# A smaller DMA scratch area and another SBUF layout in a macaron GLA / gated DeltaNet block

## The chip, the core and the metric

The kernel runs on one core of one Trainium2 chip. The metric is device time in microseconds (us). Engines are named as in the profile: PE (TensorE), DVE (VectorE), ACT (ScalarE), POOL (GpSimd), SP (SyncE); "SPq" in a chain is SP's queue, which issues most of the DMAs.

## The reference

One decoder block for 1,024 tokens and a model width of 1,024, float32:

```python
h = x + 0.5 * swiglu(rms_norm(x, ffn1_norm), ffn1_w_gate, ffn1_w_up, ffn1_w_down)   # inner width 2816
h = h + hybrid_mixer(rms_norm(h, mixer_norm), ...)    # GLA, 4 heads, and gated DeltaNet, 8 heads, merged by gates
h = h + 0.5 * swiglu(rms_norm(h, ffn2_norm), ffn2_w_gate, ffn2_w_up, ffn2_w_down)
return rms_norm(h, final_norm)
```

The DeltaNet part needs, for each head and each chunk of 64 tokens, the inverse of a unit lower triangular matrix that is made of the keys, their decays and beta.

## The kernel before

**Matmuls.** Each float32 product runs as three passes on PE over operands that are split into a high and a low part: ACT casts the high part (L119, L125), DVE or POOL subtracts the low part (L120, L126). Weights come from HBM as 128x512 tiles `raw`, and are split into `wh` and `wl` (`load_unit`, L108). The feed forwards use Strassen products over blocks of 512 (`strassen_products`, L310), whose combined activation blocks are the tiles t2h to t4l (h and l for the two parts); the activations between up and down projection are in tiles ah and al.

**Stages in the trace.** First feed forward: 0 to about 735 us. DeltaNet, one head after the other: to about 1370 us. GLA: to about 1865 us. Output projection, second feed forward and final norm: to the end.

**One DeltaNet head.** The masked, decayed key products are put into `lt` (L905 to L914) and go to DRAM as `l_d` (SP, L914), and come back in a layout with 128 blocks of 32x32 (SP, L917). POOL inverts them by 31 steps of a multiply and a subtract (L924, L927), copies the transpose (L929), and stores both to DRAM tensor `x_d` by eight DMAs that it issues itself:

```python
        for a in range(4):
            r, c = slice(32 * a, 32 * a + 32), slice(8 * a, 8 * a + 8)
            nc.gpsimd.dma_start(out=x_d[0, :, :, c], in_=xp[r])
            nc.gpsimd.dma_start(out=x_d[1, :, c, :], in_=xt[r])
```

L932 stores a 32-partition part of `xp` so that each run of contiguous bytes in `x_d` is 8 floats, 32 bytes: 1,024 runs, 32 KB. L933 stores as many bytes in runs of 8x32 floats, 1 KB: 32 runs. SP then loads them as `xb` and `yb` (L944, L945), and PE goes on from 32x32 to 64x64 blocks (`delta_levels`, L972). SP's queue holds, behind these loads, the ones of the next head: `gb` (L840, that head's cumulated decays, from `g_d`), two `raw` tiles, and `eye` into `xp` (L919). From `gb` comes the decay matrix `em` (L837 on), from that `l_d`.

**Other DMAs that POOL issues.** Eight stores of the residual to `h_d` after the first feed forward (L702), and eight loads from it before the output projection (L1356), 128 runs of 4 KB each.

**SBUF and order.** Tiles lie in pools on a stack with two ends. From the left: `const`, `xn` (normed activations), `wp` (raw x2, wh x4, wl x4), and then per stage other pools: h1 (the residual ha) and t1 (all else of the first feed forward); `me`, mx and on the right mp, sp, mb, ma in the mixer; h2 (h0 to h7) and t2 for the second feed forward. A tile that is first written where an earlier pool's tiles lay waits for the last users of just those tiles (`reuse_waits="tile"`). The order of each engine's instructions is set by a scheduler from priorities and from these waits, so that another layout can give another order.

**At the start of the mixer** POOL clears n1, xb, yb (L769) and yi (L1195); DVE and ACT copy a first projection from PSUM into yi (L1197, L1198); DVE forms the decays of all heads in yi by 16 scans of 64 tokens (L773, called at L1217), and SP stores them as `g_d` (L1219). **At its end** the loads of h0 to h7 (L1356) go to addresses of the closed mixer pools, and DVE adds the output projection to h (L281).

Of the kernel before, what the change touches and what calls it, by code (L numbers as in the profile page):

```python
# [7 lines left out]
F32 = mybir.dt.float32  # L8
F32R = mybir.dt.float32r
# [6 lines left out]
P = 128  # L16
T = 1024
# [31 lines left out]
def tile_macaron_hybrid(  # L49
# [20 lines left out]
    dram = ctx.enter_context(tc.tile_pool(name="dram", bufs=1, space=DRAM))  # L70
    xn = ctx.enter_context(tc.tile_pool(name="xn", bufs=1))
    wp = ctx.enter_context(tc.tile_pool(name="wp", bufs=4))

    nc.scalar.preload_act_table_set("sqrt_and_others")
    cs = const.tile([P, C_TRI], F32, name="cs")
# [32 lines left out]
    def load_unit(src, keep=None, stage=None):  # L108
        res = []
        for hf in range(2):  # L110
            raw = stage() if stage else wp.tile([P, 512], F32, name="raw", tag="raw", bufs=2)
            nc.sync.dma_start(out=raw, in_=src[:, hf * 512:hf * 512 + 512])
            if keep is None:
                wh = wp.tile([P, 512], F32R, name="wh", tag="wh")
                wl = wp.tile([P, 512], F32R, name="wl", tag="wl")
            else:
                wh, wl = keep[:, 0, hf], keep[:, 1, hf]
            with tc.high_priority(offset=400):
                nc.scalar.copy(out=wh, in_=raw)  # L119
# [187 lines left out]

    recent = []

    def strassen_products(tp, xs, tmp, corner, raws, place=bank, pool_steps=3):  # L310
        comb = {}

        def tile512(n):
# [1 line left out]

        def sums_own():
            for c in ("t2", "t3", "t4"):
                comb[c] = [tp.tile([P, 4, 512], F32R, name=c + p, tag=c + p) for p in "hl"]
            for k in range(4):
                def join(out, r, sl, eng):  # L320
                    eng.tensor_add(out=out, in0=xs[r][0][:, sl].bitcast(F32), in1=xs[r][1][:, sl].bitcast(F32))
                    return out

                b12 = join(corner(), k, HI, nc.vector)
                b22 = join(tile512("c11"), k + 4, HI, nc.vector)
                b11 = join(tile512("c21"), k, LO, nc.vector)
# [94 lines left out]

        return sums_own, sums_inplace, strassen

    def ffn(h, xs, wg, wu, wd, tp, ysc, first, last, pre, steps, after):
        def act_tiles():
            return [tp.tile([P, T], F32R, name=n, tag=n, bufs=2) for n in ("ah", "al")]

        def gate_up(j):
            gps, ups = ptile(), ptile()
            if j == 0:  # L430
                dense_pair(((gps, load_unit(wg[j]), P), (ups, load_unit(wu[j], stage=stage), P)), xs, first, pre, steps,
                           ((4,), (1, 5)), len(first) - 1)
            else:
                dense(gps, load_unit(wg[j]), xs)
                dense(ups, load_unit(wu[j]), xs)
            a = s_tile(tp)
            if j == 0:
                b = tp.tile([P, T], F32, name="al", tag="al", bufs=2)
                with tc.high_priority(offset=400):
                    nc.scalar.copy(out=a, in_=gps)  # L440
                    nc.scalar.copy(out=b, in_=ups)
                gps, ups = a, b
            nc.vector.tensor_mul(out=a, in0=ysc, in1=gps)
            nc.scalar.activation(out=a, in_=a, func=AF.Silu)
            nc.vector.tensor_mul(out=a, in0=a, in1=ysc)
            done[:] = [nc.vector.tensor_mul(out=a, in0=a, in1=ups).ins]
            nc.sync.dma_start(out=a_d[j], in_=a)
# [5 lines left out]
            return tp.tile([P, 512], F32, name="sr", tag="sr", bufs=2)  # L453

        def raws():
            return ([wp.tile([P, 512], F32, name="raw", tag="raw", bufs=2) for _ in range(2)] +
                    [stage() for _ in range(2)])

        def weight_sum():
            return tp.tile([P, 512], F32, name="wt", tag="wt", bufs=2)  # L460

        sums_own, sums_inplace, strassen = strassen_products(tp, xs, weight_sum, weight_sum, raws, pool_steps=2)

        def gate_up2(j):
            ss = [s_tile(tp), s_tile(tp)]
# [59 lines left out]
        def chunk_ops(c):  # L525
            names = ("b11", "b21", "t2", "t3", "t1", "t4", "b22")
            res = {}
            for i, n in enumerate(names):
                if c % 2:
                    res[n] = [[t[:, k] for k in range(2)] for t in  # L530
                              (xn.tile([P, 2, 512], F32R, name=f"x{p}{i}", tag=f"x{p}{i}") for p in "hl")]
                elif i < 6:
                    m = ("t2h", "t2l", "t3h", "t3l", "t4h", "t4l")[i]
                    t = tp.tile([P, 4, 512], F32R, name=m, tag=m)
                    res[n] = [[t[:, 2 * p + k] for k in range(2)] for p in range(2)]
                else:
                    res[n] = [[tp.tile([P, 512], F32R, name=m, tag=m, bufs=bf) for m, bf in q]
                              for q in ((("c11", 1), ("c21", 1)), (("c22", 1), ("wt", 2)))]
            return res

        def prepare(c, ops, first=None):
            parts = [first] if first else []
            for k in range(len(parts), 2):
                ss = [tp.tile([P, T], F32, name=n, tag=n, bufs=2) for n in (("ah", "al") if k and c else ("s", "s"))]
                for i in range(2):
                    nc.sync.dma_start(out=ss[i], in_=a_d[DCH[c][2 * i + k]])
                parts.append(ss)
# [1 line left out]
                yield from part_steps(k, parts[k], ops)  # L549

        def down(u, ops, h0, h1, steps):
            r1 = wp.tile([P, 512], F32, name="raw", tag="raw", bufs=2)
            r2 = tp.tile([P, 512], F32, name="sr", tag="sr", bufs=2)
            for i, t in enumerate((r1, r2)):
                nc.sync.dma_start(out=t, in_=u[:, i * 512:i * 512 + 512])
# [54 lines left out]
        sums_own()  # L610
        gate_up(1)
        with tc.issue_after(done[0]):
            at = [tp.tile([P, T], F32, name="ah", tag="ah", bufs=2) for _ in range(2)]
            for i in range(4):
                sums_inplace(i, lambda eng: at[i % 2][:, (LO, HI)[i // 2]])
        for j in range(2, NF - 4, 2):
# [19 lines left out]
        acts = []  # L636
        kept = []
        for n in ("t2h", "t2l"):
            t = tp.tile([P, 4, 512], F32R, name=n, tag=n).rearrange("p (j a) t -> p j (a t)", j=2)
# [7 lines left out]
        prev = (tail, acts)  # L647
        sqrt_table()
        ns = norm_space(tp)
        held = hold(wd, prev[0], tp)  # L650
        for seg in last:
            accumulate(wd, *prev, h, 0.5, seg, held=held)
            after(seg, ns)
# [6 lines left out]
        return st.enter_context(tc.tile_pool(name=name, bufs=bufs, reuse_waits="tile", **kw))  # L660

    with ExitStack() as st:
        hp = pool(st, "h1")
        tp = pool(st, "t1")
        ha = hp.tile([P, KT, T], F32, name="ha")
# [24 lines left out]
        def between(seg, ns):  # L690
            steps = norm_steps(h, seg, P_MX, xs2, ns)
            if seg[0] == 0:
# [6 lines left out]
        ffn(h, xs, g1, u1, d1, tp, ysc, FIRST, HALVES, begin1, None, between)  # L699
        with tc.high_priority(offset=-4000):  # L700
            for k in range(KT):
                nc.gpsimd.dma_start(out=h_d[:, k], in_=ha[:, k])  # L702

    with ExitStack() as st:
        with ExitStack() as stm:
            ys, h = mixer(stm, st, tc, pool, start, xs2, load_unit, dense, ptile, bank, rsqrt_newton, split, new_x,
                           accumulate, block_units(OBLOCKS), dram, pr, ident, ones, cst, eye, wlr, win,
                           wout, y_d, h_d, sqrt_table, strassen_products, wp, psum, divide, recent, pinned, run)
# [4 lines left out]
        held = hold(wout, units, tp)  # L713
# [20 lines left out]
        ffn(h, xs, g2, u2, d2, tp, ysc, HALVES, LAST, None, steps, finish)  # L734


def mixer(st, sto, tc, pool, start, xs, load_unit, dense, ptile, bank, rsqrt_newton, split, new_x, accumulate,
          ounits, dram, pr, ident, ones, cst, eye, wlr, win, wout, y_d, h_d, sqrt_table, strassen_products, wp, psum, divide, recent, pinned, run):
    nc = tc.nc
    mp = pool(st, "mp", side="right")  # L740
    sp = pool(st, "sp", 3, side="right")
# [503 lines left out]
    for i in range(8):  # L1245
# [28 lines left out]
        if i < 4:  # L1274
            nc.sync.dma_start(out=y_d[ORDER[i]], in_=outs[i])
    sums_own, sums_inplace, strassen = strassen_products(
        mx, xs, lambda: wp.tile([P, 512], F32, name="raw", tag="raw", bufs=2),
        lambda: wp.tile([P, 512], F32, name="raw", tag="raw", bufs=2),
        lambda: [mx.tile([P, 512], F32, name="sr", tag="sr", bufs=4) for _ in range(4)],
        lambda: psum("m", 512), 2)  # L1280
    sums_own()
# [68 lines left out]
        split(raw[t], *ys[t])  # L1350
    str_.close()
    stl.close()
    hp = pool(sto, "h2")
    h = [hp.tile([P, T], F32, name=f"h{k}", tag=f"h{k}") for k in range(KT)]
    for k in range(KT):
        nc.gpsimd.dma_start(out=h[k], in_=h_d[:, k])  # L1356
    accumulate(wout, ounits[0], ys[:4], h, 1.0)
    sqrt_table()
    return ys, h


def _units(w):
# [83 lines left out]
```

## Time and profile before

| | |
|---|---|
| median of 3 runs | 2672.56 us (2671.76 to 2674.8) |
| profiled execution, its own time | 2674.82 us |
| its span in the trace | 2672.4 us |
| PE busy | 2503.4 us, 94% of the span |
| DVE, ACT, POOL busy | 70%, 40%, 42% |

The span is what the trace covers; the execution's own time is 2.4 us longer. Engines overlap, so their shares don't add up. The chain of waits follows the last instruction back to what released it, step by step, and so tells which work set the time.

### The profile page before, as it was taken

To read this page: it belongs to the slowest core of one execution; us is meant where nothing else is said; L and a number is where in the kernel's file an instruction comes from. 1 tells how busy PE (TensorE), PEld (TensorE's weight loads), DVE (VectorE), ACT (ScalarE), POOL (GpSimd) and SP (SyncE) were. 2 spreads that over 40 slices of the span, in tenths; PEclk is the share of its full clock that TensorE was granted. 3 is DMA by queue.
4 is the path that set the end of the run, shared out by engine and by line. 5 is a ranking of instruction groups with operands and counts; after the bars stand their busy time and mean duration, and the time that the engine had idled before them with its cause. 6 is when DMAs were issued, how large, how long until landed. Compare 5 with 4: busy or idle time off the path is not lost.

```text
span 2672.4 us, 32776 instructions
## 1 busy us (share of the span) xinstructions
PE 2503.4 (94%) x11656; PEld 2019.5 (76%) x11656; DVE 1869.0 (70%) x2907; ACT 1066.5 (40%) x1845; POOL 1113.9 (42%) x1200
## 2 busy tenths in 40 slices
PE   7899999899997988889989999999989999998998
PEld 6788888667776767667767787877768888886677
DVE  8755556999686767667586757766586555558996
ACT  5333334333352434344345544545233333343331
POOL 4544444653327444445452212221154444446541
PEclk9999999999998999999999999999999999999999
DMA  3222221322222222212211212122312222213222
GB/s 114 79 73 82 83 91 60 112 79 91 98 81 52 60 56 59 60 48 56 63 50 37 80 43 84 40 84 87 122 32 76 68 87 87 87 60 115 79 87 80
DMA packets 118051, 199.04 MB, mean 74 GB/s; under 512 B 37208, under 2 KB 43096, under 8 KB 117888
## 3 DMA queue, kind: packets, MB, share of 16 engines
q1 hardware_dynamic: 111376, 184.04, 21.5%
q0 software_dynamic: 4352, 10.49, 1.5%
q10 hardware_dynamic: 2160, 2.43, 0.3%
q8 instruction: 91, 1.49, 0.2%
q14 instruction: 72, 0.59, 0.1%
HBM read 158.73 MB, written 38.17 MB: 74 GB/s over the span
## 4 chain that ended last, share of the span: by engine, by line
PE 60%; DVE 16%; POOL 9%; issue 5%; DMA 4%; ACT 4%; SPq 2%; POOLq 0%; DVEq 0%; ACTq 0%
PE q L367 28%; PE m L367 10%; PE ps L138 10%; PE q L573 6%; POOL xp L927 4%; POOL itmp L924 3%; DVE wl L126 3%; DVE xl L126 1%; DVE ha L578 1%; DVE h L578 1%; PE q L902 1%; PE q L981 1%; DMA s<-a_d 1%; DVE xl L238 1%; DMA gb<-g_d 1%
## 5 line engine op out<-in xcount | busy, mean ns | idle before, releaser
L126 DVE TENSOR_TENSOR wl<-raw,wh 128x512 fp32r<-128x512 f32 x244 | 200.2, 821 | 172.0 <-ACT wh L125 170.5
L138 PE MATMUL ps<-xl,wh 128*128 128x512 f32 (+2 forms) x736 | 254.8, 405 | 20.2 <-ACT wh L119 8.3
L126 DVE TENSOR_TENSOR wl<-sr,wh 128x512 fp32r<-128x512 f32 x232 | 204.7, 882 | 76.2 <-ACT wh L125 75.9
L138 PE MATMUL ps<-xh,wh 128*128 128x512 f32 (+2 forms) x736 | 254.4, 405 | 0.0
L138 PE MATMUL ps<-xh,wl 128*128 128x512 f32 (+2 forms) x736 | 254.2, 403 | 0.1
L367 PE MATMUL q<-xh,wl 128*128 128x512 f32 x640 | 249.4, 390 | 0.0
L367 PE MATMUL q<-xh,wh 128*128 128x512 f32 x640 | 249.3, 390 | 0.0
L367 PE MATMUL q<-xl,wh 128*128 128x512 f32 x640 | 249.2, 389 | 0.0
L125 ACT CAST wh<-sr 128x512 fp32r<-128x512 f32 x232 | 143.7, 619 | 244.7 <-PE q L573 61.9
L924 POOL TENSOR_TENSOR itmp<-lt,xp 128x112 f32<-128x112 f32 (+29 forms) x248 | 114.9, 463 | 255.1 <-DMA lt<-l_d 226.1
L472 POOL TENSOR_TENSOR s<-s,ysc 128x512 f32<-128x512 f32 x80 | 112.6, 1418 | 247.8 <-ACT s L471 247.8
L125 ACT CAST wh<-raw 128x512 fp32r<-128x512 f32 x244 | 144.9, 594 | 176.2 <-PE q L367 100.5
L138 PEld LDWEIGHTS ps<-xl,wh 128*128 128x128 f32 (+1 forms) x736 | 137.8, 191 | 51.7 <-DVE xl L238 9.1
L355 POOL TENSOR_TENSOR raw<-sr 128x512 f32<-128x512 f32 x20 | 27.5, 1375 | 328.6 <-DMA sr<-in_win 235.8
L138 PEld LDWEIGHTS ps<-xh,wh 128*128 128x128 f32 (+1 forms) x736 | 138.8, 192 | 24.6 <-issue 0.8
L138 PEld LDWEIGHTS ps<-xh,wl 128*128 128x128 f32 (+1 forms) x736 | 137.4, 191 | 23.7 <-issue 1.0
L378 DVE TENSOR_TENSOR c<-c,q 128x512 f32<-128x512 f32 x120 | 82.4, 686 | 84.8 <-PE q L367 84.6
L367 PEld LDWEIGHTS q<-xl,wh 128*128 128x128 f32 x640 | 120.2, 188 | 26.2
L367 PEld LDWEIGHTS q<-xh,wl 128*128 128x128 f32 x640 | 120.1, 188 | 25.5
L367 PEld LDWEIGHTS q<-xh,wh 128*128 128x128 f32 x640 | 120.1, 188 | 25.3
L373 ACT COPY c<-q 128x512 f32<-128x512 f32 x120 | 70.5, 588 | 162.2 <-PE q L367 161.7
L927 POOL TENSOR_TENSOR xp<-xp,itmp 128x112 f32<-128x112 f32 (+29 forms) x248 | 120.9, 488 | 19.4
(483 smaller groups left out, 6780.8 us busy)
## 6 DMA issues: line engine op xcount, KB each, us to landing
sr<-in_win SPq DMA_DIRECT2D x80, 256.0 KB, 2.6
a_d<-s SPq DMA_DIRECT2D x36, 512.0 KB, 3.7
raw<-in_win SPq DMA_DIRECT2D x66, 256.0 KB, 2.6
raw<-in_d SPq DMA_DIRECT2D x56, 256.0 KB, 2.6
raw<-in_g SPq DMA_DIRECT2D x48, 256.0 KB, 2.6
s<-a_d SPq DMA_DIRECT2D x24, 512.0 KB, 4.2
sr<-in_u SPq DMA_DIRECT2D x44, 256.0 KB, 2.7
raw<-in_u SPq DMA_DIRECT2D x44, 256.0 KB, 2.6
```

What stands on the lines that cost most here:

```text
L125: a = nc.scalar.copy(out=hi, in_=src)
L126: b = (eng or nc.vector).tensor_sub(out=lo, in0=src, in1=hi.bitcast(F32))
L138: mm = nc.tensor.matmul(out=ps[:m, sl], lhsT=w[:, :m], rhs=x[:, sl], start=(i == 0 and a == 0), stop=(i == n - 1 and a == 2))
L355: nc.gpsimd.tensor_tensor(out=o, in0=a, in1=b, op=op)
L367: nc.tensor.matmul(out=ps, lhsT=p[:, c], rhs=q, start=(first and k == 0 and a == 0), stop=(k == 3 and a == 2), skip_group_check=not first)
L373: marks[0] = nc.scalar.copy(out=t, in_=ps).ins
L378: marks[1] = nc.vector.tensor_add(out=t, in0=t, in1=ps).ins
L472: nc.gpsimd.tensor_mul(out=s, in0=s, in1=y)
L573: nc.tensor.matmul(out=ps, lhsT=p[:, c], rhs=q, start=(first and k == 0 and a == 0), stop=(k == 1 and a == 2), skip_group_check=not first)
L578: nc.vector.scalar_tensor_tensor(out=hd[:, sl], in0=ps, scalar=0.5, in1=hd[:, sl], op0=ALU.mult, op1=ALU.add)
L924: inv_eng.tensor_tensor(out=tv, in0=lp[:, j, j + 1:].unsqueeze(2).broadcast_to([P, r, m]), in1=xp[:, j, :m].unsqueeze(1).broadcast_to([P, ...
L927: inv_eng.tensor_tensor(out=xv, in0=xv, in1=tv, op=ALU.subtract)
```

## The change

Three things:

- The two `raw` tiles move from the left end (`wp`) to a new pool `rp` at the right end.
- The tiles t2h to t4l, ah and al of both feed forwards move from t1 and t2 into new pools q1 and q2 (`tq`), which are opened before h1 and h2. They then lie directly above `wp`, and ha or h0 to h7 above them.
- The program is built with `dynamic_dma_scratch_size=2048`, where the default is 16384. This is an area at the bottom of each SBUF partition which is kept for DMAs that POOL issues. Everything on the left moves down by 14,336 bytes.

In the mixer `me` now covers what t2h to t4l, ah and al left, and the right-hand pools with yi cover what ha left. Between the mixer's left and right pools 12 KB per partition are now covered by neither; h0 to h2 lie there.

```diff
     wp = ctx.enter_context(tc.tile_pool(name="wp", bufs=4))
+    rp = ctx.enter_context(tc.tile_pool(name="rp", bufs=2, side="right"))
...
-            raw = stage() if stage else wp.tile([P, 512], F32, name="raw", tag="raw", bufs=2)
+            raw = stage() if stage else rp.tile([P, 512], F32, name="raw", tag="raw", bufs=2)
...
-                comb[c] = [tp.tile([P, 4, 512], F32R, name=c + p, tag=c + p) for p in "hl"]
+                comb[c] = [(tq or tp).tile([P, 4, 512], F32R, name=c + p, tag=c + p) for p in "hl"]
...
-            return [tp.tile([P, T], F32R, name=n, tag=n, bufs=2) for n in ("ah", "al")]
+            return [tq.tile([P, T], F32R, name=n, tag=n, bufs=2) for n in ("ah", "al")]
...
     with ExitStack() as st:
+        tq = pool(st, "q1")
         hp = pool(st, "h1")
...
     stl.close()
+    tq = pool(sto, "q2")
     hp = pool(sto, "h2")
...
-    nc = _bacc.Bacc("TRN2", target_bir_lowering=False, num_devices=1)
+    nc = _bacc.Bacc("TRN2", target_bir_lowering=False, num_devices=1, dynamic_dma_scratch_size=2048)
```

Line numbers of the changed kernel are larger by 1 to 4 (L702 is L705 there, L769 L772, L773 L776, L914 L917, L917 L920, L932 L935, L1195 L1198, L1356 L1360). The order of instructions is the same on all engines but for the program's first 80 us and the first heads of the mixer. ACT has two rows more, both loads of its function tables.

POOL where the mixer starts, before: the memsets of three tiles that were cleared at L769 (one of them, n1, is printed as n_5770) and of yi stand behind the last stores of the residual and the last splits (xl) of the normed activations.

```order
L702 DMA h_d<-ha 128x1024 x3
L126 TENSOR_TENSOR xl_5419<-c_5224,xh_5418 128x512
L126 TENSOR_TENSOR xl_5429<-c_5226,xh_5428 128x512
L126 TENSOR_TENSOR xl_5439<-c_5225,xh_5438 128x512
L126 TENSOR_TENSOR xl_5449<-c_5224,xh_5448 128x512
L769 MEMSET n_5770 128x1024
L769 MEMSET xb 128x1024
L769 MEMSET yb 128x1024
L1195 MEMSET yi 128x1024
L924 TENSOR_TENSOR itmp<-lt,xp 128x31
```

And now:

```order
L705 DMA h_d<-ha 128x1024 x2
L772 MEMSET n_5777 128x1024
L772 MEMSET xb 128x1024
L772 MEMSET yb 128x1024
L705 DMA h_d<-ha 128x1024
L127 TENSOR_TENSOR xl_5425<-c_5230,xh_5424 128x512
L127 TENSOR_TENSOR xl_5435<-c_5232,xh_5434 128x512
L127 TENSOR_TENSOR xl_5445<-c_5231,xh_5444 128x512
L127 TENSOR_TENSOR xl_5455<-c_5230,xh_5454 128x512
L1198 MEMSET yi 128x1024
L927 TENSOR_TENSOR itmp<-lt,xp 128x31
```

The three memsets stand ahead of the last store and the last splits; yi's comes right behind the splits.

DVE some 10 us later, before: the last of the 16 scans into yi (L773), between rows of the first head's convolution (acc, kq).

```order
L773 SCALAR_TENSOR_TENSOR yi<-cs,oT 8x64 x12
L120 TENSOR_TENSOR wl<-raw,wh 128x512
L791 SCALAR_TENSOR_TENSOR acc<-ps,ph,acc 128x511
L773 SCALAR_TENSOR_TENSOR yi<-cs,oT 8x64
L791 SCALAR_TENSOR_TENSOR acc<-ps,ph,acc 128x510
L773 SCALAR_TENSOR_TENSOR yi<-cs,oT 8x64
L791 SCALAR_TENSOR_TENSOR acc<-ps,ph,acc 128x509
L773 SCALAR_TENSOR_TENSOR yi<-cs,oT 8x64 x2
L1231 TENSOR_SCALAR beta<-q 128x8x4
```

And now, the last 11 rows up to the last scans (L776):

```order
L776 SCALAR_TENSOR_TENSOR yi<-cs,oT 8x64 x6
L830 SCALAR_TENSOR_TENSOR kq_5789<-sig,acc 128x4x128
L794 SCALAR_TENSOR_TENSOR acc<-ps,ph,acc 128x512
L776 SCALAR_TENSOR_TENSOR yi<-cs,oT 8x64
L794 SCALAR_TENSOR_TENSOR acc<-ps,ph,acc 128x512
L776 SCALAR_TENSOR_TENSOR yi<-cs,oT 8x64
L794 SCALAR_TENSOR_TENSOR acc<-ps,ph,acc 128x512
L121 TENSOR_TENSOR wl<-raw,wh 128x512
L776 SCALAR_TENSOR_TENSOR yi<-cs,oT 8x64 x3
L830 SCALAR_TENSOR_TENSOR kq_5789<-sig,acc 128x4x128
L776 SCALAR_TENSOR_TENSOR yi<-cs,oT 8x64 x2
```

The scans are spread over more of the convolution's rows: ahead of the last of them stand rows (acc, kq, wl) which stood behind it.

SP behind the store of the decays (`g_d`), before:

```order
L1219 DMA g_d<-yi 8x1024
L840 DMA gb<-g_d 128x1024 x2
L112 DMA raw<-in_win 128x512 x2
L914 DMA l_d_6018<-em 32x8x32 x4
L112 DMA raw<-in_win 128x512
L917 DMA lt<-l_d_6018 32x1024 x4
```

And now:

```order
L1222 DMA g_d<-yi 8x1024
L843 DMA gb<-g_d 128x1024 x2
L113 DMA raw<-in_win 128x512
L917 DMA l_d_6025<-em 32x8x32 x4
L113 DMA raw<-in_win 128x512 x2
L920 DMA lt<-l_d_6025 32x1024 x4
```

The weights' `raw` loads stand elsewhere: one before the store of `l_d` and two between it and the loads of `lt`, where there were two and one.

## Rows read from the trace of the kernel before

**Rows 1.** The page: PE's busy time (part 1) and the chain by engine (part 4).
```profile
PE 2503.4 (94%) x11656; PEld 2019.5 (76%) x11656; DVE 1869.0 (70%) x2907; ACT 1066.5 (40%) x1845; POOL 1113.9 (42%) x1200
...
PE 60%; DVE 16%; POOL 9%; issue 5%; DMA 4%; ACT 4%; SPq 2%; POOLq 0%; DVEq 0%; ACTq 0%
```

**Rows 2.** Windows, one delta head: us, then busy us (instructions) per engine, PEclk, DMA share, GB/s.
```profile
1019.00:1089.00 70.00, 63.07 (x344) 50.99 (x343) 51.81 (x112) 30.02 (x57) 35.82 (x72) 0.98 0.22 57
```

**Rows 3.** Chain of waits, 944 to 1036 us: start us, us, what.
```profile
947.90 1.02 POOL xt L929
...
952.50 2.95 DMA x_d<-xp
...
961.10 5.03 DMA gb<-g_d
...
974.17 2.13 DVE em L908 x8
...
1023.13 2.67 DMA x_d<-xp
```

**Rows 4.** Timeline of POOL, 946 to 954 us: start us, us, engine, line, operation.
```profile
948.75 0.78 POOL L932 DMA_DIRECT2D x_d<-xp  x1
949.52 0.50 POOL L933 DMA_DIRECT2D x_d<-xt  x1
...
952.50 0.87 POOL L932 DMA_DIRECT2D x_d<-xp  x1
```

**Rows 5.** Lines L932 and L933: ns min/median/max to issue; last, time to landing.
```profile
L932 POOL DMA_DIRECT2D x_d<-xp x32: 759/806/871, 823.8 to 1299.6; - x32
...
DMA to landing us min/median/max: 2.6/2.7/4.4
...
L933 POOL DMA_DIRECT2D x_d<-xt x32: 502/540/615, 824.6 to 1300.3; - x32
...
DMA to landing us min/median/max: 2.0/2.1/3.9
```

**Rows 6.** Chain of waits near x_d of heads 1, 2, 7, 8.
```profile
827.64 2.72 DMA x_d<-xp
...
877.95 0.69 PE ps L138 x3
...
1233.36 0.70 DVE h L1038
...
1299.58 2.73 DMA x_d<-xp
```

**Rows 7.** Timelines of POOL and DVE, and waits of PE, 740 to 748 us.
```profile
742.55 0.96 POOL L1195 MEMSET yi<- 128x1024 f32 x1
...
743.55 0.69 DVE L1197 COPY yi<-ps 72x512 f32<-72x512 f32 x1 [0.67 <-POOL yi L1195]
...
PE ps L138 <- ACT yi L1198: 1.3, 1, 1.3
```

**Rows 8.** Timelines of SP and POOL, 760 to 791 us.
```profile
762.80 0.34 SPq L1219 DMA_DIRECT2D g_d<-yi  x1
...
778.61 1.82 SPq L914 DMA_DIRECT2D l_d<-em  x4
...
782.72 1.70 SPq L917 DMA_DIRECT2D lt<-l_d  x4
...
787.61 0.24 POOL L924 TENSOR_TENSOR itmp<-lt,xp 128x31 f32<-128x31 f32 x1 [44.10 <-DMA lt<-l_d]
```

**Rows 9.** Timelines of POOL, DVE and PE, 1872 to 1882 us.
```profile
1875.12 4.29 POOL L1356 DMA_DIRECT2D h<-h_d  x8 [26.94 <-DVE xl L126]
...
1879.44 1.22 DVE L281 SCALAR_TENSOR_TENSOR h<-ps,h 128x1024 f32<-128x1024 f32 x1 [2.59 <-DMA h<-h_d]
...
1880.82 0.70 PE L138 MATMUL ps<-xl,wh 128*128 128x512 f32 x2 [2.77 <-DVE h L281]
```

**Rows 10.** ACT's table loads at L1209, in the groups by line.
```profile
L1209 ACT ACT_TABLE_LOAD x1 | 1.3, 1283 | 0.0
```

More of the change, by code (lines that the diff above doesn't have):

```diff
@@ L308, in tile_macaron_hybrid, with strassen_products @@
     recent = []
-    def strassen_products(tp, xs, tmp, corner, raws, place=bank, pool_steps=3):
+    def strassen_products(tp, xs, tmp, corner, raws, place=bank, pool_steps=3, tq=None):
         comb = {}
@@ L422, in strassen_products, with ffn @@
         return sums_own, sums_inplace, strassen
-    def ffn(h, xs, wg, wu, wd, tp, ysc, first, last, pre, steps, after):
+    def ffn(h, xs, wg, wu, wd, tq, tp, ysc, first, last, pre, steps, after):
         def act_tiles():
-            return [tp.tile([P, T], F32R, name=n, tag=n, bufs=2) for n in ("ah", "al")]
+            return [tq.tile([P, T], F32R, name=n, tag=n, bufs=2) for n in ("ah", "al")]
         def gate_up(j):
@@ L437, in gate_up @@
             if j == 0:
-                b = tp.tile([P, T], F32, name="al", tag="al", bufs=2)
+                b = tq.tile([P, T], F32, name="al", tag="al", bufs=2)
                 with tc.high_priority(offset=400):
@@ L455, in raws @@
         def raws():
-            return ([wp.tile([P, 512], F32, name="raw", tag="raw", bufs=2) for _ in range(2)] +
+            return ([rp.tile([P, 512], F32, name="raw", tag="raw", bufs=2) for _ in range(2)] +
                     [stage() for _ in range(2)])
@@ L460, in weight_sum @@
             return tp.tile([P, 512], F32, name="wt", tag="wt", bufs=2)
-        sums_own, sums_inplace, strassen = strassen_products(tp, xs, weight_sum, weight_sum, raws, pool_steps=2)
+        sums_own, sums_inplace, strassen = strassen_products(tp, xs, weight_sum, weight_sum, raws, pool_steps=2, tq=tq)
         def gate_up2(j):
@@ L533, in chunk_ops @@
                     m = ("t2h", "t2l", "t3h", "t3l", "t4h", "t4l")[i]
-                    t = tp.tile([P, 4, 512], F32R, name=m, tag=m)
+                    t = tq.tile([P, 4, 512], F32R, name=m, tag=m)
                     res[n] = [[t[:, 2 * p + k] for k in range(2)] for p in range(2)]
@@ L543, in prepare @@
             for k in range(len(parts), 2):
-                ss = [tp.tile([P, T], F32, name=n, tag=n, bufs=2) for n in (("ah", "al") if k and c else ("s", "s"))]
+                ss = [p.tile([P, T], F32, name=n, tag=n, bufs=2)
+                      for p, n in (((tq, "ah"), (tq, "al")) if k and c else ((tp, "s"), (tp, "s")))]
                 for i in range(2):
@@ L551, in down @@
         def down(u, ops, h0, h1, steps):
-            r1 = wp.tile([P, 512], F32, name="raw", tag="raw", bufs=2)
+            r1 = rp.tile([P, 512], F32, name="raw", tag="raw", bufs=2)
             r2 = tp.tile([P, 512], F32, name="sr", tag="sr", bufs=2)
@@ L612, in ffn @@
         with tc.issue_after(done[0]):
-            at = [tp.tile([P, T], F32, name="ah", tag="ah", bufs=2) for _ in range(2)]
+            at = [tq.tile([P, T], F32, name="ah", tag="ah", bufs=2) for _ in range(2)]
             for i in range(4):
@@ L638, in ffn @@
         for n in ("t2h", "t2l"):
-            t = tp.tile([P, 4, 512], F32R, name=n, tag=n).rearrange("p (j a) t -> p j (a t)", j=2)
+            t = tq.tile([P, 4, 512], F32R, name=n, tag=n).rearrange("p (j a) t -> p j (a t)", j=2)
             kept.append([t[:, k] for k in range(2)])
@@ L649, in ffn @@
         ns = norm_space(tp)
-        held = hold(wd, prev[0], tp)
+        held = hold(wd, prev[0], tq)
         for seg in last:
@@ L698, in between @@
                        steps=steps)
-        ffn(h, xs, g1, u1, d1, tp, ysc, FIRST, HALVES, begin1, None, between)
+        ffn(h, xs, g1, u1, d1, tq, tp, ysc, FIRST, HALVES, begin1, None, between)
         with tc.high_priority(offset=-4000):
@@ L705, in tile_macaron_hybrid @@
         with ExitStack() as stm:
-            ys, h = mixer(stm, st, tc, pool, start, xs2, load_unit, dense, ptile, bank, rsqrt_newton, split, new_x,
+            ys, h, tq = mixer(stm, st, tc, pool, start, xs2, load_unit, dense, ptile, bank, rsqrt_newton, split, new_x,
                            accumulate, block_units(OBLOCKS), dram, pr, ident, ones, cst, eye, wlr, win,
-                           wout, y_d, h_d, sqrt_table, strassen_products, wp, psum, divide, recent, pinned, run)
+                           wout, y_d, h_d, sqrt_table, strassen_products, rp, psum, divide, recent, pinned, run)
         tp = pool(st, "t2")
@@ L712, in tile_macaron_hybrid @@
         units = block_units(OBLOCKS)[1]
-        held = hold(wout, units, tp)
+        held = hold(wout, units, tq)
         ysc = tp.tile([P, T], F32, name="ysc", tag="ysc")
@@ L732, in finish @@
                 (nc.sync if k % 2 else nc.scalar).dma_start(out=out[k, :, sl], in_=o)
-        ffn(h, xs, g2, u2, d2, tp, ysc, HALVES, LAST, None, steps, finish)
+        ffn(h, xs, g2, u2, d2, tq, tp, ysc, HALVES, LAST, None, steps, finish)
 def mixer(st, sto, tc, pool, start, xs, load_unit, dense, ptile, bank, rsqrt_newton, split, new_x, accumulate,
-          ounits, dram, pr, ident, ones, cst, eye, wlr, win, wout, y_d, h_d, sqrt_table, strassen_products, wp, psum, divide, recent, pinned, run):
+          ounits, dram, pr, ident, ones, cst, eye, wlr, win, wout, y_d, h_d, sqrt_table, strassen_products, rp, psum, divide, recent, pinned, run):
     nc = tc.nc
@@ L1276, in mixer @@
     sums_own, sums_inplace, strassen = strassen_products(
-        mx, xs, lambda: wp.tile([P, 512], F32, name="raw", tag="raw", bufs=2),
-        lambda: wp.tile([P, 512], F32, name="raw", tag="raw", bufs=2),
+        mx, xs, lambda: rp.tile([P, 512], F32, name="raw", tag="raw", bufs=2),
+        lambda: rp.tile([P, 512], F32, name="raw", tag="raw", bufs=2),
         lambda: [mx.tile([P, 512], F32, name="sr", tag="sr", bufs=4) for _ in range(4)],
@@ L1358, in mixer @@
     sqrt_table()
-    return ys, h
+    return ys, h, tq
 def _units(w):
```

## Prediction

> **What bounds the kernel now.** I read the page first: PE is busy for 94% of the span, but the chain that ended last lies on PE for 60% alone [rows 1]. So there are stretches in which something else sets the time, and a transfer or a wait there counts in full. Then I went by windows along the span. In one DeltaNet head of 70 us PE works 63.1 us and POOL 35.8 us [rows 2]: nobody is full, which is how a closed loop looks. The chain of waits shows the loop [rows 3]: POOL ends the inverse and copies the transpose; POOL issues the eight stores to x_d; the last `xp` store takes 2.95 us to land; SP, which waits for it, issues the loads of xb and yb and only behind them `gb` of the next head, 5.03 us; DVE makes `em`; `l_d` and `lt` go through DRAM; POOL inverts again, and about 70 us after the one landing stands the next. Every delay on POOL or at a landing is then a delay of the next head.
>
> The chain also holds the x_d landings of the heads 1 and 8, and, with the same rows as these, 3 to 6; at head 2 it runs through PE, at head 7 through DVE and ACT [rows 6]. So six of the eight heads pass their delay on, and two have slack of a size that the chain does not show.
>
> **The scratch area.** The change cuts by eight what SBUF holds for DMAs that POOL issues. The rows tell that POOL writes something for each piece of such a DMA: L932 and L933 move 32 KB each, one in 1,024 runs of 32 bytes, the other in 32 runs of 1 KB, and cost POOL 806 and 540 ns [rows 5]. With the large area nothing waits for room. The four L932 of a head start 1.25 us apart (948.75 to 952.50 in three steps [rows 4]), while each needs 2.7 us to land [rows 5], so at each start but the first one or two others are still under way. No row shows what POOL does when room runs out. Bounds:
>
> - Nothing waits, because the pieces still fit: 0.
> - An L932 waits until the L932 before it has landed: four starts 2.7 us apart instead of 1.25, so the last one starts 3 x 1.45 = 4.35 us later. Call it 4.3 us per head.
> - Every one of the eight waits for the one before: three pairs of 2.7 + 2.1 us and one L932 until the last L933 starts, 17.1 us after the first start instead of 4.6: 12.5 us per head.
>
> I take the middle. L932 is by far the finest cut of POOL's transfers: 1,024 runs over 16 DMA engines are 64 for each, and 2,048 bytes are 32 bytes for each of these 64. If a piece takes more than 16 of them, the area holds one L932 and not two, and the second has to wait for the first, as the chosen case has it; at less, two fit, the first is nearly home when the third starts (2.7 us against 2 x 1.25), and nothing waits. That a piece needs a source, a target and a length makes the first the likelier to me. L933 brings two runs per engine and takes hardly any room, so it need not wait for itself. Six heads make 6 x 4.3 = 25.8 us; with bounds of 0 and, with all eight heads, 34.4 us (the third bullet, 6 x 12.5 = 75 us, I leave outside as unlikely).
>
> [...]
>
> POOL's other transfers, L702 and L1356, have eight runs per engine, 128 of 4 KB over 16, and I cost them at nothing: the stores of h_d are waited for much later, and the loads fall under the next but one part.
>
> **The start of the mixer.** In the trace POOL clears three tiles and then yi at 742.55, DVE waits 0.67 us for that, and PE 1.3 us for ACT's copy into yi [rows 7]. Now the three memsets come ahead of the last splits, and yi's stands 2.7 us earlier (three memsets of about 0.9 us). That gain holds only if yi sets what comes next. What it leads to is the decays: scans, `g_d` at 762.80, `l_d` at 778.61, `lt` at 782.72, POOL's first inverse at 787.61 [rows 8]. In the changed order DVE puts several convolution rows ahead of the last scans, and SP puts two `raw` loads instead of one between `l_d` and `lt`, the second of which needs DVE's split of an older tile. I walked the changed DVE rows with the durations of before and got the last scan 4 to 5 us later than now; I take 4.5 us, with bounds of -2.7 us (the early yi carries through) and +5 us. That goes into the first head's loop, on which the landing at 827.64 of [rows 6] lies, in full. ACT's two further table loads, at 1.28 us each [rows 10], are one before the first norm's square root and one ahead of the first tanh here, where ACT has room; 0, at most 1.3 us for each.
>
> **The end of the mixer.** POOL issues the eight loads of h only at 1875.12, after waiting 26.94 us for a split on DVE whose input lay on the same addresses; h0 lands some 4 us later, DVE adds at 1879.44 and PE, which waits for the freed PSUM, stands for 2.77 us [rows 9]. Now h0 to h2 lie where neither pool of the mixer lay, and their loads wait for nothing there. DVE can add as soon as its last split is done (1876.85, the 1879.44 less the 2.59 us it waited). Gain 2.6 us, with bounds of 0 (the next load or the order of DVE eats it) and 2.8 us. The loads come earlier beside others that have several us to spare; I cost that at nothing, and should it fail, the bound of 0 is it.
>
> All the rest keeps its order: the Strassen products of both feed forwards, the heads from the fourth on, GLA, and the final norm. Moving `raw` to the other end changes no count of buffers.
>
> **The sum.** The profiled execution took 2674.8 us, 2.4 more than its span, and 2.3 more than the median of the runs. 2674.8 + 25.8 + 4.5 - 2.6 = 2702.5; against the median 2672.6 that is 2700.3. I predict **2700 us** for a median. This case's own range: at least five heads (21.5) with nothing lost at the start and 2.8 gained at the end, 2691; at most eight heads (34.4), 5 at the start, two table loads (2.6) and no gain at the end, 2714.6, of which I give 2713.
>
> **Rivals.** A measurement of this kernel tells about 0.2%, 5.3 us, from no change.
>
> - *The pieces still fit, or POOL writes ahead without waiting.* Then only the ends of the mixer count: 2672.6 + 4.5 - 2.6 = 2674.5, no change. For it: no row shows POOL short of room. Against: the eightfold cut, and fine-cut stores that overlap now. Chance 0.24.
> - *Faster: yi sets the first head.* If the pieces fit and DVE, which idles at 743 waiting for yi [rows 7], gets through the convolution rows in the time that it wins, the first inverse starts 2.7 us earlier and the end of the mixer gives 2.8: 2667.1. It decides on whether the last scan ends before the 762.80 of `g_d` [rows 8]. It is just over the 0.2%. Chance 0.12.
> - *The stores wait, but most heads have slack.* If the chain is one of two about equally long paths, PE's 63.1 of 70 us [rows 2] being the other, a late landing is partly absorbed: three heads of 4.3 and the sum of the ends give 2672.6 + 12.9 + 1.9 = 2687.4. Chance 0.14.
> - *Forecast*, 2700: chance 0.50.
>
> So slower 0.64, same 0.24, faster 0.12. The range takes in the three other cases as far as needed, from 2668 to 2713; outside lie some of the fastest case and every DMA waiting for the one before.
>
> **What would show it.** Right: in the changed profile the starts of L932 (there L935) lie about 2.7 us apart, POOL's time for the second to fourth of a head grows from 0.8 to some 2 us or idle time stands ahead of them, and the heads last about 74 us instead of 70; the loads of h0 to h2 start tens of us before 1875 and PE's 2.77 us are gone; POOL's first inverse starts after 790. Wrong: L932 starts still 1.25 us apart (the first rival), an unchanged period of the heads in spite of late stores (the third), or a first inverse before 787 (the second).

## The result, and the profile after

| | before | after |
|---|---|---|
| median of 6 runs, us | 2673.41 (2671.35 to 2680.51) | 2698.94 (2695.04 to 2708.34) |
| ratio to before, 95% interval | | 1.0097 (1.0076 to 1.0117) |
| profiled execution: span, us | 2672.4 | 2699.9 |

The changed kernel is 25.5 us slower, against the 0.2% (5.3 us) that can be told from no change. The forecast was 2700. The time agrees, but two of the terms behind it were wrong, in opposite directions, as the experiments show.

The page of the changed kernel, beside [rows 1]: PE's busy time is the same, its share lower, and the chain has the same parts.

```profile
PE 2504.6 (93%) x11656; PEld 2029.9 (75%) x11656; DVE 1877.7 (70%) x2907; ACT 1069.9 (40%) x1847; POOL 1110.5 (41%) x1200
...
PE 61%; DVE 14%; POOL 8%; issue 5%; ACT 4%; DMA 4%; SPq 1%; POOLq 0%; DVEq 0%; ACTq 0%
```

The stores to x_d in the changed kernel's timeline of POOL, which answers to [rows 4]:

```profile
1026.10 0.79 POOL L935 DMA_DIRECT2D x_d<-xp  x1
1026.88 0.50 POOL L936 DMA_DIRECT2D x_d<-xt  x1
1029.09 0.76 POOL L935 DMA_DIRECT2D x_d<-xp  x1 [1.71 <-issue]
...
1035.02 0.76 POOL L935 DMA_DIRECT2D x_d<-xp  x1 [1.73 <-issue]
```

They start 2.98 us apart instead of 1.25, and the idle time in brackets has no releaser ("issue"). From the fourth head on the inverses start about 75 us after each other, where it was 70. The line's own view, as in [rows 5], sums it up:

```profile
L935 POOL DMA_DIRECT2D x_d<-xp x32: 754/766/823, 827.9 to 1332.6; - x32
...
  issue: 42.4, 24
...
DMA to landing us min/median/max: 2.6/2.6/3.7
```

POOL stands still 24 times, three times for each of eight heads, for 42.4 us in all. One landing takes 2.6 us; POOL goes on about 0.35 us after it. The chain of waits now has idle pieces between the x_d stores, which follow each other without idle time in [rows 4] (start us, us, what):

```profile
1027.38 1.71 issue
1029.09 0.76 POOL x_d L935
...
1035.02 2.64 DMA x_d<-xp
```

At the start of the mixer, the changed kernel's timelines of POOL and of SP (compare [rows 7] and [rows 8]):

```profile
737.43 0.95 POOL L1198 MEMSET yi<- 128x1024 f32 x1
...
791.28 0.79 POOL L927 TENSOR_TENSOR itmp<-lt,xp 128x31 f32<-128x31 f32 x1 [52.90 <-DMA lt<-l_d]
```

```profile
766.02 0.34 SPq L1222 DMA_DIRECT2D g_d<-yi  x1
...
782.73 3.47 SPq L113 DMA_DIRECT2D raw<-in_win  x2
786.39 1.73 SPq L920 DMA_DIRECT2D lt<-l_d  x4
```

yi is cleared 5.1 us earlier (2.7 us by its new place, the rest because the first feed forward ends earlier), but `g_d` goes out 3.2 us later, and the first inverse starts 3.7 us later. At the end of the mixer (timelines of POOL and of DVE, compare [rows 9]):

```profile
1885.31 2.17 POOL L1360 DMA_DIRECT2D h<-h_d  x4
1907.09 2.15 POOL L1360 DMA_DIRECT2D h<-h_d  x4 [19.61 <-ACT xh L126]
```

```profile
1911.70 2.35 DVE L127 TENSOR_TENSOR xl<-oG,xh 128x1024 fp32r<-128x1024 f32 x2
1913.97 1.22 DVE L282 SCALAR_TENSOR_TENSOR h<-ps,h 128x1024 f32<-128x1024 f32 x1
```

The first four h loads start 26 us ahead of the last splits on DVE (the xl rows of oG), and the add of h0 follows these without the 2.59 us of waiting that [rows 9] shows.

And something that the prediction did not have. Three Strassen products of a feed forward are 252 matmuls; the texts below call such a stretch a product. Here are windows of the same stretch, before and after (columns as in [rows 2]):

```profile
150.22:208.10 57.88, 57.88 (x253) 47.30 (x253) 30.26 (x42) 20.38 (x35) 24.28 (x17) 1.00 0.28 91
```

```profile
151.01:208.13 57.12, 57.12 (x253) 47.30 (x252) 30.82 (x42) 20.36 (x35) 23.83 (x17) 1.00 0.29 93
```

PE is full in both, does the same work, with the same count of matmuls in the records, at the full granted clock (1.00), and takes 0.76 us less. The same holds for the next two stretches and for one of the second feed forward.

### The profile page after: what moved, and what is told of

The parts are those of the page before. It is cut to its first block, busy times and chain, and to the rows that moved or that the text cites. A ratio compares the mean times of both kernels' runs of the same rounds, so it can differ in the third digit from the quotient of the medians.

```text
span 2699.9 us, 32774 instructions
## 1 busy us (share of the span) xinstructions
PE 2504.6 (93%) x11656; PEld 2029.9 (75%) x11656; DVE 1877.7 (70%) x2907; ACT 1069.9 (40%) x1847; POOL 1110.5 (41%) x1200
## 4 chain that ended last, share of the span: by engine, by line
PE 61%; DVE 14%; POOL 8%; issue 5%; ACT 4%; DMA 4%; SPq 1%; POOLq 0%; DVEq 0%; ACTq 0%
PE q L368 27%; PE ps L139 11%; PE m L368 10%; PE q L575 6%; POOL xp L930 3%; POOL itmp L927 3%; DVE wl L127 2%; PE q L984 1%; DVE xl L127 1%; DVE h L580 1%; DVE ha L580 1%; DMA gb<-g_d 1%; DMA s<-a_d 1%; PE q L905 1%; PE ps L1146 1%
## 5 line engine op out<-in xcount | busy, mean ns | idle before, releaser
L127 DVE TENSOR_TENSOR wl<-raw,wh 128x512 fp32r<-128x512 f32 x244 | 208.4, 854 | 167.9 <-ACT wh L126 166.4
L368 PEld LDWEIGHTS q<-xl,wh 128*128 128x128 f32 x640 | 120.1, 188 | 25.8 <-issue 0.8
```

The source lines that it names most:

```text
L127: b = (eng or nc.vector).tensor_sub(out=lo, in0=src, in1=hi.bitcast(F32))
L368: nc.tensor.matmul(out=ps, lhsT=p[:, c], rhs=q, start=(first and k == 0 and a == 0), stop=(k == 3 and a == 2), skip_group_check=not first)
```

## The experiments

Theory A: with 2,048 bytes, an L932 store waits until the one before has landed. Rival B: the time goes to the new order and layout.

**1. The changed kernel with 4,096 bytes of scratch.** Its order is the changed kernel's on every engine.

```diff
-    nc = _bacc.Bacc("TRN2", target_bir_lowering=False, num_devices=1, dynamic_dma_scratch_size=2048)
+    nc = _bacc.Bacc("TRN2", target_bir_lowering=False, num_devices=1, dynamic_dma_scratch_size=4096)
```

> The changed kernel with the scratch area at 4096 bytes instead of 2048; the order of all engines is that of the changed kernel, every address is 2048 bytes higher. Theory A (an x_d store waits until the one before has left room): with twice the area three pairs fit, the four stores of xp start 1.25 us apart again instead of 2.98, and the 5.2 us per head go: 2699 - 6 to 8 heads x 4.5 to 5.2 us = 2658 to 2672 us. Rival B (the time is lost by the new order at the start of the mixer and by the layout, the stores' wait is hidden): 2695 to 2703 us. The two weights of the feed forwards: one product of the Strassen loop takes 57.12 us here as in the changed kernel if the place of raw matters, and may go back to 57.88 us if the low address does.

Measured: 2655.15 us, ratio to before 0.9931 (0.9916 to 0.9946). In its timeline of POOL the stores start about 1.25 us apart (first and fourth shown) and never wait:

```profile
825.12 0.81 POOL L935 DMA_DIRECT2D x_d<-xp  x1
...
828.92 0.86 POOL L935 DMA_DIRECT2D x_d<-xp  x1
```

So theory A holds, and the scratch area alone costs 2698.94 - 2655.15 = 43.8 us: about the 42.4 us of idle on POOL, so little of it is hidden. The time lies below the 2658 to 2672 us expected: all the rest of the change is a gain of 0.7%, which neither this expectation nor the prediction foresaw.

**2. The changed kernel with the default of 16,384 bytes.** The same edit with that number; some rows of the first 80 us and of the mixer's start change places.

> The changed kernel with the scratch area at its default of 16384 bytes, so that h0 to h2 lie again where the mixer's pools lie. Theory A: the stores start 1.25 us apart, as in the run with 4096 bytes, and 30 us go; PE's gap at the first add to h (2.8 us) comes back: 2661 to 2675 us. Rival B: 2695 us or more. For the 57.12 us of a Strassen product: 57.12 if it comes from raw's place, 57.88 if it comes from the lower addresses.

Measured: 2656.88 us, 0.9929 (0.9912 to 0.9947), below the range expected too, stores 1.27 us apart. Low addresses are not what speeds up the Strassen products: they take 57.12 us here too. And the 2.8 us at the first add to h did not come back, though h0 to h2 lie on the mixer's pools again: most loads of h go out ahead of DVE's last splits, and the add of h0 does not wait (timelines of POOL and of DVE).

```profile
1867.04 2.66 POOL L1360 DMA_DIRECT2D h<-h_d  x5 [21.19 <-ACT xh L126]
```

```profile
1873.92 1.21 DVE L282 SCALAR_TENSOR_TENSOR h<-ps,h 128x1024 f32<-128x1024 f32 x1
```

**3. The kernel before with 2,048 bytes.** Only the number is added to its `Bacc` line.

> The kernel before with the scratch area at 2048 bytes and nothing else. Theory A: the stores of xp start 2.98 us apart, and six to eight heads lose 4.3 to 5.2 us: 2699 to 2715 us, more than the changed kernel has if the faster Strassen products come from raw's place (57.88 us here), about as much if they come from the lower addresses (57.12 us here). Rival B: 2668 to 2679 us.

Measured: 2724.98 us, 1.0191 (1.0175 to 1.0207). The view of its line L932 (idle time before it, us and times):

```profile
  issue: 44.0, 24
```

POOL waits 24 times for 44.0 us, and the whole loss is 50 us, above the range expected. The rest is there before the first store: this kernel too has another order in the first 80 us and at the start of the mixer, and its first inverse starts at 796.2 us instead of 787.6; 2.4 us of that are lost before the mixer begins. The products take 57.88 us.

**4. The kernel before with the raw tiles at the right end.**

```diff
+    rp = ctx.enter_context(tc.tile_pool(name="rp", bufs=2, side="right"))
...
-            raw = stage() if stage else wp.tile([P, 512], F32, name="raw", tag="raw", bufs=2)
+            raw = stage() if stage else rp.tile([P, 512], F32, name="raw", tag="raw", bufs=2)
...
```

(The other places that take a raw tile change in the same way.)

> The kernel before with only the raw weight tiles at the right end. If a Strassen product's 57.12 us come from there, 2673 less about 9 us, 2661 to 2667 us, with 57.12 us per product; if not, 57.88 us and 2670 to 2677 us. Theory A: the stores start 1.25 us apart, as before.

Measured: 2673.01 us, 0.9994 (0.9984 to 1.0004): no change, and 57.88 us per product:

```profile
150.29:208.17 57.88, 57.88 (x253) 47.30 (x253) 30.25 (x42) 20.38 (x35) 24.60 (x17) 1.00 0.28 91
```

The raw tiles' place does nothing, so the gain came with the tiles t2h to t4l, ah and al.

Where within a product it lies is seen in the starts of PE's matmuls, in the kernel before (timeline of PE):

```profile
163.12 0.39 PE L367 MATMUL q<-xh,wh 128*128 128x512 f32 x1
163.34 0.39 PE L367 MATMUL q<-xl,wh 128*128 128x512 f32 x1
163.57 0.39 PE L367 MATMUL q<-xh,wl 128*128 128x512 f32 x1
...
165.84 0.40 PE L367 MATMUL q<-t2h,wh 128*128 128x512 f32 x1
166.08 0.39 PE L367 MATMUL q<-t2l,wh 128*128 128x512 f32 x1
166.31 0.40 PE L367 MATMUL q<-t2h,wl 128*128 128x512 f32 x1
166.55 0.39 PE L367 MATMUL q<-t2h,wh 128*128 128x512 f32 x1
```

Matmuls on the activations xh and xl start about 0.227 us apart, those on t2h and t2l 0.23 and 0.24 by turns, 0.233 on average over a block of twelve. By the addresses in the built program xh, xl, wh and wl of this kernel start 256 bytes behind a multiple of 512 (the first wh at 87,808), and the t tiles 384 behind one (the first t2h at 171,904): the small tiles nv and ny of the norm, 128 bytes in all, lie ahead of them. In the changed kernel they lie directly above the weights and have the weights' offset.

**5. The kernel before with 128 more bytes in nv and ny.** Its order is the same on every engine.

```diff
-        nv, ny = ([tp.tile([P, 8], F32, name=n, tag=n, bufs=2) for _ in range(2)] for n in ("nv", "ny"))
+        nv, ny = ([tp.tile([P, 16], F32, name=n, tag=n, bufs=2) for _ in range(2)] for n in ("nv", "ny"))
...
-    nc = _bacc.Bacc("TRN2", target_bir_lowering=False, num_devices=1)
+    nc = _bacc.Bacc("TRN2", target_bir_lowering=False, num_devices=1, dynamic_dma_scratch_size=15872)
```

> The kernel before, with the order of all engines unchanged; the small tiles nv and ny of the norm get 64 instead of 32 bytes, so that t2h to t4l, ah and al of both feed forwards, which lie behind them, start at multiples of 256 bytes instead of 128 bytes behind one; the scratch area is 15872 instead of 16384 bytes, to make room. Theory C (a matmul's operand that starts 128 bytes off a multiple of 256 is read slower): a Strassen product of the feed forwards takes 57.12 us instead of 57.88, each matmul on a t tile 0.227 instead of 0.233 us, and the kernel about 2674 - 12 = 2657 to 2667 us. Rival D (it is the tiles' place near the weights, or what lies beside them): 57.88 us and 2669 to 2679 us.

Measured: 2662.75 us, 0.9957 (0.9942 to 0.9972), and 57.12 us per product:

```profile
150.22:207.34 57.12, 57.12 (x254) 47.30 (x253) 30.79 (x42) 20.38 (x35) 24.46 (x18) 1.00 0.27 92
```

An offset of 128 bytes was worth 11 us of the kernel before.

**6. The changed kernel with 2,560 bytes of scratch.**

> The changed kernel with a scratch area of 2560 bytes, all else and the order the same. If a piece takes 16 bytes, 160 fit for each DMA engine: two stores of xp and two of xt fit (about 136), a third store of xp has to wait for the first, which has landed by then or nearly so. The second start is 1.25 us behind the first, the third near 3 us, the last about 4.3 us instead of 9: 2699 - 8 x 4.7 = 2657 to 2668 us. If a piece takes 32 bytes or more, only one store of xp fits as with 2048: starts 2.98 us apart, 2694 to 2705 us.

Measured: 2661.11 us, 0.995 (0.9936 to 0.9965). The starts in the timeline of POOL:

```profile
826.44 0.81 POOL L935 DMA_DIRECT2D x_d<-xp  x1
...
827.75 0.81 POOL L935 DMA_DIRECT2D x_d<-xp  x1
...
829.46 0.76 POOL L935 DMA_DIRECT2D x_d<-xp  x1 [0.41 <-issue]
...
830.75 0.76 POOL L935 DMA_DIRECT2D x_d<-xp  x1
```

The second store of `xp` no longer waits, the third waits 0.41 us for the first, the fourth not again; in all heads together POOL waits 9 times, for 5.9 us. Just 512 bytes more take away most of the loss. As an estimate from these runs: two stores of `xp`, with a store of `xt` between them, do not fit in 2,048 bytes and fit in 2,560, so one store of `xp` takes at most 1,280 bytes of the area, and with a store of `xt` more than 1,024. In the division that was expected, 64 pieces for each DMA engine, 1,280 bytes are 20 for a piece; pieces of 32 bytes would have left the second store waiting. No run shows how the area is divided.

**7 and 8. The changed kernel with 4,096 bytes, everything on the left shifted by 128 or by 256 bytes.**

```diff
+    pad = const.tile([P, 32], F32, name="pad")
     cs = const.tile([P, C_TRI], F32, name="cs")
```

(64 elements in the second.)

> The changed kernel with 4096 bytes of scratch, and a tile of 128 bytes at the bottom that nothing uses: all tiles of the left end, the normed activations, the weights' parts and t2h to t4l, start 128 bytes behind a multiple of 256. Theory C: all matmuls of the Strassen products take 0.233 instead of 0.227 us, a product 59.7 instead of 57.12 us, and the kernel 20 to 55 us more than with 4096 bytes alone (2655): 2675 to 2710 us. Rival D: 2650 to 2660 us.

> As the last one with 256 bytes: the tiles start at multiples of 512 instead of 256 behind one. If multiples of 256 are all that counts, 57.12 us per product and 2650 to 2660 us. [...]

Measured: 2656.72 us, 0.9936 (0.9921 to 0.995), and 2654.95 us, 0.9926 (0.9912 to 0.9939): the time of experiment 1, at 57.12 us per product. With 128 bytes:

```profile
152.46:209.58 57.12, 57.12 (x253) 47.31 (x252) 30.83 (x43) 20.37 (x35) 24.22 (x17) 1.00 0.27 93
```

Theory C falls in this form: tiles may all start at odd multiples of 128. What is left is the offset of a matmul's two operands against each other.

**9. The changed kernel with 4,096 bytes, weights and t tiles shifted against xh and xl.**

```diff
     wp = ctx.enter_context(tc.tile_pool(name="wp", bufs=4))
+    wpad = wp.tile([P, 32], F32, name="pad", tag="pad", bufs=1)
```

> The changed kernel with 4096 bytes of scratch, and 128 unused bytes between the normed activations and the weights' parts: wh, wl and the t tiles behind them are shifted by 128 bytes, xh and xl are not. Theory C2 (a matmul is slower where its two operands' starts differ by an odd multiple of 128 bytes, whichever they are; from the run with all shifted by 128, which lost nothing): now the matmuls on xh and xl take 0.233 us and those on t tiles 0.227, the opposite of the kernel before; a Strassen product takes 57.12 + 148 x 0.0065 = 58.1 us; with the dense products of the mixer, which are all on xh and xl, 2675 to 2700 us. Rival D2 (only the place of the t tiles matters): 57.12 us and 2650 to 2660 us.

Measured: 2677.21 us, 1.0011 (0.9997 to 1.0024), 22 us above experiment 1, and a product takes 58.12 us, where 58.1 were worked out (with 148 matmuls on xh and xl; it has 144):

```profile
151.83:209.95 58.12, 58.12 (x253) 47.30 (x252) 30.61 (x42) 20.38 (x35) 24.41 (x17) 1.00 0.27 91
```

Its timeline of PE shows the kernel before turned round: xh and xl 0.23 and 0.24 us apart by turns, t2h and t2l about 0.227.

```profile
165.73 0.40 PE L369 MATMUL q<-xl,wh 128*128 128x512 f32 x1
165.97 0.39 PE L369 MATMUL q<-xh,wl 128*128 128x512 f32 x1
166.20 0.40 PE L369 MATMUL q<-xh,wh 128*128 128x512 f32 x1
...
168.28 0.39 PE L369 MATMUL q<-t2h,wh 128*128 128x512 f32 x1
168.51 0.39 PE L369 MATMUL q<-t2l,wh 128*128 128x512 f32 x1
168.74 0.39 PE L369 MATMUL q<-t2h,wl 128*128 128x512 f32 x1
```

**10. The scans at a higher priority** (4,096 bytes).

```diff
-    seg_scan(sm[64:72], gtm, ones[64:72, :64])
+    with tc.high_priority(offset=400):
+        seg_scan(sm[64:72], gtm, ones[64:72, :64])
```

> The changed kernel with 4096 bytes of scratch, and the 16 scans of the decays at a higher priority, so that they stand in one piece on DVE as the first 12 did in the kernel before; the order of the first heads changes with it. If the scattered scans set the first head's start, POOL's first inverse starts near 782 us instead of 788.5 and, passed on whole, 2648 to 2651 us. If other work of the first three heads sets the time by then, 2653 to 2660 us, with the later heads where they are with 4096 bytes alone.

Measured: 2652.83 us, 0.9923 (0.9906 to 0.994), between the two ranges expected. POOL's first and fourth inverse in experiment 1, and here:

```profile
788.52 0.29 POOL L927 TENSOR_TENSOR itmp<-lt,xp 128x31 f32<-128x31 f32 x1 [53.41 <-DMA lt<-l_d]
...
976.35 0.23 POOL L927 TENSOR_TENSOR itmp<-lt,xp 128x31 f32<-128x31 f32 x1 [25.27 <-DMA lt<-l_d]
```

```profile
783.89 0.24 POOL L927 TENSOR_TENSOR itmp<-lt,xp 128x31 f32<-128x31 f32 x1 [47.32 <-DMA lt<-l_d]
...
976.33 0.23 POOL L927 TENSOR_TENSOR itmp<-lt,xp 128x31 f32<-128x31 f32 x1 [26.71 <-DMA lt<-l_d]
```

The first starts 4.6 us earlier, the fourth at the same time, the fifth to the eighth about 2 us earlier. So the scattered scans did cost the first head some us, and the next heads take most of it back. The 2.3 us between the medians are less than the intervals can tell, and what gives the 2 us of the later heads was not tried.

**11. The stores of the transposed inverse issued by SP** (4,096 bytes).

```diff
-            nc.gpsimd.dma_start(out=x_d[1, :, c, :], in_=xt[r])
+            nc.sync.dma_start(out=x_d[1, :, c, :], in_=xt[r])
```

> The changed kernel with 4096 bytes of scratch, and the stores of the transposed inverse (L936) issued by SP instead of POOL. POOL's four stores of xp then start 0.8 us apart, the fourth a little later for want of room (near 3 us behind the first instead of 3.75), and POOL is free 2 us earlier. If the landing of x_d is what the next head waits for, 0.8 us per head and 2646 to 2652 us; if SP, which then waits for POOL ahead of other loads, holds back weights or the next head's matrix, 2656 to 2680 us.

Measured: 2668.24 us, 0.9984 (0.9972 to 0.9996), 13 us above experiment 1. SP's timeline at the first x_d:

```profile
828.81 1.73 SPq L936 DMA_DIRECT2D x_d<-xt  x4
830.63 1.53 SPq L917 DMA_DIRECT2D l_d<-em  x3
...
838.76 0.45 SPq L917 DMA_DIRECT2D l_d<-em  x1
```

A part of the next head's `l_d` stands behind the loads of xb and yb now. Its second, third and fourth inverse start at 846.9, 921.9 and 994.6 us, 5, 11 and 18 us after those of experiment 1. But 4 us of that are there at the first inverse already (792.4 against 788.5), ahead of every store that was changed, so they are not its work. Whether the store of `l_d` or the weights' loads in SP's queue hold back more was not tried.

POOL's stores of `xp` start 0.8 us apart now, and though the area has 4,096 bytes, POOL waits before the fourth in each of the eight heads (the view of L935, idle time before it):

```profile
  issue: 8.1, 8
```

That fits the estimate of experiment 6: three stores of at most 1,280 bytes fit in 4,096, and as the fourth does not, a store of `xp` takes more than 1,024 by itself.

## Why the prediction was right, and where its terms were not

The place where the changed kernel loses most was named, and the mechanism is shown by experiments 1, 3, 6 and 11: a store of `xp` waits for room until an earlier one has landed, with 2,048 bytes three times per head. That the sum came out is luck: two misses cancel, and two terms lie above the bounds that the prediction gave them (34.4 us for the stores, 5 us for the start of the mixer).

| term | predicted, us | measured, us | from |
|---|---|---|---|
| stores to x_d | +25.8 | +43.8 | medians, with 2,048 against 4,096 bytes |
| start of the mixer | +4.5 | +6.8, given back by the fourth head | traces, before against experiment 1 |
| end of the mixer | -2.6 | -2.7 | the same |
| feed forwards | 0 | -11 | medians, before against experiment 5 |

The measured terms, with the 8.2 us that the heads give back, add up to 29 us, against the 25.5 of the medians; the intervals leave 4 to 5 us open either way on each median.

**The stores, mis-sized.** Per head the term was 3 x 1.45 = 4.35 us; it is 3 x (2.98 - 1.25) = 5.2 us, since POOL goes on only 0.35 us after the landing. And the step "six of the eight heads pass their delay on" fell: eight heads of 5.2 us are 41.6, and the medians say 43.8. Between the traces of experiment 1 and of the changed kernel, the starts of the inverses move apart by 4.8, 2.1, 4.5, 5.2, 5.2, 4.5 and 6.3 us from head to head, and by some 7 behind the last. So head 2 did have the slack that the chain suggested [rows 6], some 3 us of it; head 7 had none, though the chain ran through DVE and ACT there. A chain shows one of several paths of nearly the same length, and says nothing of how far behind the others are. In all, the heads lose 39.5 us between the two traces, whose spans differ by 45.4 us. Of the rest 3.3 us lie in the first feed forward, where POOL stores nothing to x_d: from 470 to 510 us the granted clock is 0.91 in the changed kernel's trace, with short times at half of the full clock (0.50 from 474 to 476 us), and 1.00 in that of experiment 1. So a few of the 43.8 us may be the clock's and not the stores'.

The choice that an area of 2,048 bytes holds one L932 and not two was right, but by a narrow margin: it asked for pieces of more than 16 bytes, and experiment 6, where two stores of 64 pieces each fit, allows at most 2,560 / 128 = 20. That the area is shared out by pieces for each DMA engine was the author's assumption. No run shows it; as an estimate from the runs, a whole store of `xp` takes more than 1,024 bytes (experiment 11) and at most 1,280 (experiment 6).

**The start of the mixer, right in its place and too small.** By a split on DVE near the end of the first feed forward (first row before, second row experiment 1) the kernel of experiment 1 is 5.9 us ahead:

```profile
522.52 1.77 DVE L126 TENSOR_TENSOR xl<-ah,xh 128x512 fp32r<-128x512 f32 x1
```

```profile
516.67 1.72 DVE L127 TENSOR_TENSOR xl<-ah,xh 128x512 fp32r<-128x512 f32 x1
```

At the first inverse it is 0.9 us behind (788.52 against 787.61 in [rows 8]), so the stretch costs 6.8 us where 4.5 were walked. A part may be the granted clock: from 735 to 790 us it is 0.94 in experiment 1 and 1.00 before. But at the fourth it is 7.3 us ahead (976.35 above, and before):

```profile
983.69 0.23 POOL L924 TENSOR_TENSOR itmp<-lt,xp 128x31 f32<-128x31 f32 x1 [29.83 <-DMA lt<-l_d]
```

The heads 2 to 4, whose order changes too, give 8.2 us back. The prediction costed those heads at nothing ("All the rest keeps its order" begins with the fourth); experiment 10, which moved the scans and left the fourth head where it was, fits with other work that sets the time there, though its later heads are 2 us earlier. Which of the moved rows gives the gain was not tried.

**The end of the mixer, right in size.** Experiment 1 is 7.1 us ahead at the last GLA products (DVE's L378 at 1865.22 us before) and 9.8 at the add of h0: 2.7 us. But the prediction gave as the reason that h0 to h2 now lie where neither pool of the mixer lay. Experiment 2 has no such free place, and its add does not wait either. So the free place is not needed: at the new addresses above q2 most loads of h wait for a cast on ACT and not for DVE's last splits.

**The feed forwards, the step that failed.** "All the rest keeps its order", and so costs nothing, holds for order and waits, but not for durations: the prediction took each matmul's duration to be independent of its tiles' addresses. The trace of before had the hint, 0.233 against 0.227 us, in the starts of matmuls of one loop. By PE's starts experiment 1 goes from 1.4 us behind at 89 us, where the new order of the first 80 us has cost it time, to 5.7 ahead at 735, and from 10.4 ahead at 2006 us to 17.9 at the end: 7.1 and 7.5 us in the two feed forwards. As a median the shift alone gives 11.0 in experiment 5.

Without the small scratch area, the same layout is 0.7% faster than the kernel before. Experiment 1 beats both kernels; with the scans in one piece (2652.83 us) it is at least as fast.

## What to carry to other kernels

A buffer that is cut to win space has to be costed by what is in flight in it: count the pieces of the finest-cut DMAs that POOL issues and look at how close their starts stand to each other's landings. In the changed kernel POOL waited 24 times, for 42.4 us, before the stores of `xp` with 1,024 runs each, and never before those of `xt`, as many bytes in 32 runs. When a layout changes, compare the durations of the same instruction on different tiles, not the order and the waits alone. And a sum that comes out is no proof of its terms: one run with the suspected number put back showed two errors, of some 18 us in the stores and 20 in all else, that had cancelled.

## What the runs showed of the hardware that was not expected

- fp32r matmuls of 512 columns at the full granted clock took 0.227 us where the starts of moving operand and weights in SBUF differed by a multiple of 256 bytes, and 0.233 us on average, 3% more, where they differed by an odd multiple of 128: for the t tiles in the kernel before, for xh and xl in experiment 9. The place of both together did not matter: 57.12 us per product in experiments 7 and 8, as in experiment 1. Why was not tried, nor other types or offsets.
- With 2,048 bytes of scratch POOL stood still for 1.7 us after each of a head's first three pairs of stores, until the store of `xp` had landed (2.6 us after its start) and about 0.35 us longer; the profile shows that as idle time without a releaser. With 512 bytes more the first head's four stores waited once, for 0.41 us. With 4,096 bytes POOL did not wait where the stores of `xp` were 1.25 us apart (experiment 1), and waited before the fourth, 8.1 us in eight heads, where they were 0.8 us apart (experiment 11).
